# Staging the first-use weights of layer 1 in eight slots of the second residual buffer, and the flag's branch one step into the odd layer

## Chip, cores and metric

One of the eight cores of a Trainium2 chip runs the whole kernel. The metric is the device time of one execution in microseconds (us), the median of several runs. Engines are named as in the profile: PE (matrix multiplication), DVE (vector), ACT (scalar and activation), POOL (GpSimd), SP (the queue from which every DMA here is issued).

## What is computed

Two residual layers and a final norm over 2048 tokens of width 1024. Layer 0 ("even") mixes attention over the 256 keys that an index score selects with a gated convolution of 31 taps; layer 1 ("odd") is a gated convolution of 3 taps. Cut to what matters here:

```
def even_layer(h, pos, w_in, w_out, ...):
    q, k, v, qi, ki, wi, gate_a, glu_b, gate_b = _split(h @ w_in, EVEN_SPLIT)
    a = dsa_attention(rope(q), rope(k), v, rope(qi), rope(ki), wi) * silu(gate_a)
    c = silu(layer_norm(causal_depthwise_conv(g_lin * sigmoid(g_gate), cb_w))) * silu(gate_b)
    return concatenate([a, c], axis=-1) @ w_out

def odd_layer(h, w_in, conv_w, w_out):
    b_gate, c_gate, xin, gate = split(h @ w_in, 4, axis=-1)
    y = b_gate * causal_depthwise_conv(c_gate * xin, conv_w)
    return (y * silu(gate)) @ w_out

x = x + even_layer(rms_norm(x, norm_g[0]), ...)
x = x + odd_layer(rms_norm(x, norm_g[1]), ...)
return rms_norm(x, final_g)
```

## The kernel before

The tokens are worked on in four chunks of 512 (`c` = 0 to 3). A product with float32 accuracy is made of three float16 matmuls (`mm3`, lines 189 to 191): high part by high part, high by low, low by high. Each weight matrix is cut into tiles `wt` of 1024 x 256 that hold both halves; there are two `wt` buffers.

**A weight's first use.** `weight` (line 195 on) fetches a tile in four quarters of 256 KB. A quarter goes by DMA into a float32 staging tile `w_stage` (line 205, pool `stg`, two buffers), ACT scales it in place (line 210), ACT casts the high half into `wt` (line 211), and POOL subtracts to get the low half (line 212). The finished tile is also written to DRAM (line 213), and every later use is one DMA of 1 MB from there (line 199). Layer 1's input weights `wO` have 16 tiles and layer 0's output weights `woE` four; both are first used for chunk 0.

**The order of work around the change.** After layer 0's projections, gates and selection of the last chunk, the program runs for chunk 0: the last gates (`late`, lines 1122 on, in two pieces), `out_even(0)` (line 1014 on, 192 matmuls with `woE`), the norm (`norm_odd`, whose row factor `rs_d` DVE makes at line 165), and `odd(0)` (line 1050 on): 16 steps, one tile of `wO` and 48 matmuls each. `weave` runs such a main generator and, between its steps, takes so many pieces of filler generators as a rate says. Fillers are `cnv`, the 31-tap convolution of the next chunk on DVE (line 243), and `att`, the attention of the next chunk: 32 heads (4 blocks of 128 tokens, 8 heads each) and two pieces that finish the last heads, 34 pieces in all.

**One head of attention.** PE makes the scores (line 1172, `ps_q`), DVE adds the mask and takes the maximum (line 345), ACT takes the exponential (line 352) and casts (line 354), POOL subtracts (line 355, `pp`), SP issues a transposing DMA (line 357, `pt`), and PE multiplies with the values (line 378, `ps_v`). The values of a head stand two heads behind its scores.

**The branch.** All of chunk 1's attention needs the selection to be right. A flag (`fl`, `fps`, `fi`, lines 1140 to 1147) is loaded by all engines (line 1148), which branch on it (line 1149) to a slow fallback. No instruction moves across that branch. It stands after `ALONE` = 2 steps of `odd(0)`; in these steps only the convolution is woven in, and afterwards the loop at line 1186 on weaves attention at `R2` = 2.45 pieces per step into the other 14 steps.

The residual rows of a chunk, `x1` (16 KB in each partition), have two buffers in pool `l1`, used in turn; `rows` hands one out. Chunk 0 uses the first; the second stays empty until `out_even(1)`. Within what the program text allows, a scheduler orders the instructions of each engine's queue.

Of the kernel before, what the change touches and what calls it, by code (L numbers as in the profile page):

```python
# [12 lines left out]
FP32 = mybir.dt.float32  # L13
# [8 lines left out]
P = 128  # L22
S = 2048
D = 1024
KD = D // P
NB = S // P
CH = 512
# [15 lines left out]
NCAND = 16  # L43
NWT = 2
LOOK = 2
ALONE = 2
ATR = 3.5
CE, CX, CN0, CNR, R0, R1, R2 = 1.5, 3.0, 1.0, 0.85, 1.65, 1.65, 2.45
ORDER = ('ggqgqg', 'ggqgqg', 'gggg', 'qq')
EX = 1  # L50
TQ, TP = 2, 4
# [9 lines left out]
WT = 256  # L61
# [13 lines left out]
def trunk_kernel(ctx: ExitStack, tc: tile.TileContext, xT, pos, wE, woE, wO, woO, par, tab, outT):  # L75
# [40 lines left out]
    w_dr = {}  # L116
    URGENT = {(wE.tensor.name, t) for t in (T_K, T_QI, T_KI)}

    state = {"mm": None, "gate": None, "first": None, "scanned": False}

    def paced(ins):
        if state["gate"] is not None:
            tc.add_manual_dep(ins.ins, state["gate"].ins.name, mybir.DependencyInfo(mybir.DependencyClass.NoSync, mybir.DependencyReason.DATA), reason="pace")

    def drain(gen):
        for _ in gen:
            pass

    def weave(main, steps=99, *fills):
        owed = [0.0] * len(fills)  # L130
        for n, _ in enumerate(main):
            state["gate"] = state["mm"]
            for i, (gen, rate) in enumerate(fills):
                owed[i] += rate
                while owed[i] >= 1.0:
                    owed[i] -= 1.0
                    next(gen, None)
            state["gate"] = None
            if n + 1 == steps:
                break  # L140
# [13 lines left out]
    def row_rstd(pool, ps_pool, sq, inv_n, out_scale, n=TT):  # L154
        return spread(ps_pool, row_diag(pool, ps_pool, sq, inv_n, out_scale, n), n)
# [31 lines left out]
    def mm3(out, sh, sl, mh, ml):  # L187
        for k in range(KD):
            T.matmul(out=out, lhsT=sh(k), rhs=mh(k), start=k == 0, stop=False)  # L189
            T.matmul(out=out, lhsT=sh(k), rhs=ml(k), start=False, stop=False)  # L190
            state["mm"] = T.matmul(out=out, lhsT=sl(k), rhs=mh(k), start=False, stop=k == KD - 1)  # L191
        if state["first"] is None:
            state["first"] = state["mm"]

    def weight(pool, stage_pool, src, t):
        key = (src.tensor.name, t)
        wt = pool.tile([P, 2, KD, WT], F16, name="wt")
        if key in w_dr:
            SP.dma_start(out=wt, in_=w_dr[key])
            return wt  # L200
        w_dr[key] = dram.tile([P, 2, KD, WT], F16, name=f"w_{key[0]}_{t}")
        for q in range(4):
            ks = slice(2 * q, 2 * q + 2)
            st = stage_pool.tile([P, 2, WT], FP32, name="w_stage")
            SP.dma_start(out=st, in_=src[t, :, ks, :])
            if key in URGENT:
                A.activation(out=wt[:, 0, ks, :], in_=st, func=AF.Copy, scale=SW)
                paced(V.scalar_tensor_tensor(out=wt[:, 1, ks, :], in0=st, scalar=SW, in1=wt[:, 0, ks, :], op0=ALU.mult, op1=ALU.subtract))
            else:
                A.activation(out=st, in_=st, func=AF.Copy, scale=SW)  # L210
                A.copy(out=wt[:, 0, ks, :], in_=st)  # L211
                G.tensor_tensor(out=wt[:, 1, ks, :], in0=st, in1=wt[:, 0, ks, :], op=ALU.subtract)  # L212
        SP.dma_start(out=w_dr[key], in_=wt)
        return wt
# [212 lines left out]
    with ExitStack() as es:  # L427
# [482 lines left out]
        def score_slot(i, n):  # L910
            return scp.tile([P, n, CH], FP32, name=f"sc{i}", padded_shape=[P, n, -(-(NB - TT + i + 1) * P // n)])
# [34 lines left out]
        a, b, d = score_slot(3, 4), score_slot(0, 3), score_slot(1, 3)  # L946
# [6 lines left out]
        x1 = first_normalize(1, acc, held)  # L953
# [31 lines left out]
    l1 = ctx.enter_context(tc.tile_pool(name="l1", bufs=2, reuse_waits="tile"))  # L985
# [52 lines left out]
    def halves():  # L1038
        return xp.tile([P, KD, CH], F16, name="xh"), xp.tile([P, KD, CH], F16, name="xl")
# [42 lines left out]
    def out_odd(c, x1, yh, yl, parts=1):  # L1082
        acc = l1.tile([P, CH], FP32, name="ssum", bufs=1)
        w = CH // parts
        for n in range(parts):
            tok = slice(n * w, (n + 1) * w)
            for t in range(NTW):
                wt = weight(wp, stg, woO, t if n % 2 == 0 else NTW - 1 - t)
                for z in range(2):
                    jt = 2 * (t if n % 2 == 0 else NTW - 1 - t) + z  # L1090
                    zs = slice(z * P, (z + 1) * P)
                    ps = ps_w.tile([P, CH], FP32, name="ps_w")[:, 0:w]
                    mm3(ps, lambda k: wt[:, 0, k, zs], lambda k: wt[:, 1, k, zs], lambda k: yh[:, k, tok], lambda k: yl[:, k, tok])
                    x = x1[:, jt, tok]
                    V.scalar_tensor_tensor(out=x, in0=ps, scalar=1.0 / (SY * SW), in1=x, op0=ALU.mult, op1=ALU.add)
                    square_into(l1, acc[:, tok], x, t + z == 0, V)
                yield
            rb = row_rstd(l1, ps_n, acc[:, tok], 1.0 / D, 1.0, w // P)
            for k in range(0, KD, parts):
                o = l1.tile([P, CH], FP32, name="y" if parts > 1 and k // parts % 2 else "xi").rearrange("p (z t) -> p z t", z=parts)  # L1100
                for z in range(parts):
                    V.scalar_tensor_tensor(out=o[:, z, :], in0=x1[:, k + z, tok], scalar=gf[:, k + z:k + z + 1], in1=rb[:, 0:w], op0=ALU.mult, op1=ALU.mult)  # L1102
                rows = outT[k * P:(k + parts) * P, c * CH + n * w:c * CH + (n + 1) * w]
                SP.dma_start(out=rows.rearrange("(z p) t -> p z t", z=parts), in_=o)

    m = {}

    def rows():
        return l1.tile([P, KD, CH], FP32, name="x1"), l1.tile([P, CH], FP32, name="ssum", bufs=1)

    def last_gates():
        xh, xl = held_last
# [8 lines left out]

    late = last_gates()
    x1, acc = rows()
    weave(late, LG)
    for z in range(2):
        SP.dma_start(out=mix(0)[z][:, 4:8, :], in_=mc_dr[:, z])
# [6 lines left out]
    n = norm_odd(x1, acc, late)  # L1133
    drain(late)
    yh, yl = halves()
    main = odd(*n, yh, yl)
    weave(main, ALONE, (cnv, CN0))

# [54 lines left out]
    for c in range(NCH):  # L1193
        att = attend(c + 1) if c + 1 < NCH else iter(())
        if c > 0:
            cnv = conv(c + 1) if c + 1 < NCH else iter(())
            x1, acc = rows()
            weave(out_even(c, *m[c], x1, acc), 99, (cnv, CNR), (att, R0))
            n = norm_odd(x1, acc, late, (cnv, CNR), (att, R1))
            weave(late, 99, (cnv, CNR), (att, R1))  # L1200
            yh, yl = halves()
            main = odd(*n, yh, yl)
        weave(main, 99, (cnv, CNR if c else CN0), (att, R1 if c else R2))
        late = out_odd(c, x1, yh, yl, 2 if c + 1 == NCH else 1)
        drain(att)
        drain(cnv)
# [71 lines left out]
```

## Time and profile before

| | |
|---|---|
| runs | 2228.39, 2229.94, 2234.19 us; median 2229.94 |
| profiled execution | 2226.34 us, of which the profile spans 2224.6 |
| PE | 1988.8 us busy (89%), mean granted clock 0.97 |
| DVE, ACT, POOL | 1659.4 (75%), 1177.1 (53%), 803.5 us (36%) |
| `w_stage<-in_wo_dram` | 64 DMAs of 256 KB, median 3.3 us from issue to landing |
| `pt<-pp` | 320 transposing DMAs, median 3.3 us |

PE is busy for nine tenths of the span, but in the page's row of 40 slices its share falls to 7 and 8 tenths in slices 18 to 21 (about 1000 to 1220 us), which are `odd(0)` and what follows on it. A busy share is a mean over stages with different limits, so this stretch is to be read by itself: which engine waits, for what, and what lies ahead of it in the queues.

### The profile page before, as it was taken

How to read it: one execution, taken by the hardware profiler on the slowest of the kernel's cores; microseconds unless marked ns; L12 is line 12 of the kernel's file. 1: busy time of each engine (PE TensorE's matmuls, PEld its weight loads, DVE VectorE, ACT ScalarE, POOL GpSimd, SP SyncE). 2: the span in 40 equal slices, each digit the busy share in tenths (PEclk: the TensorE clock that was granted, in tenths of full speed). 3: DMA queues.
4: the chain of work that ended last, by engine and by line, in shares of the span. 5: the costliest groups of instructions: out<-in, count | busy, mean ns of one | idle time of the engine just before them, and what ended most of it. 6: DMA issues, size and time to landing. Idle time of an engine off the chain costs nothing. (4 is left out here: it accounts for less than half of the span.)

```text
span 2224.6 us, 34871 instructions
## 1 busy us (share of the span) xinstructions
PE 1988.8 (89%) x12252; PEld 1071.2 (48%) x12252; DVE 1659.4 (75%) x3485; ACT 1177.1 (53%) x2407; POOL 803.5 (36%) x761
## 2 busy tenths in 40 slices
PE   5778888888999998897877999999999999999997
PEld 4644464555464543343433444554444555444446
DVE  7999969998988867887662887875788887343224
ACT  5666666566567855465673564554455567121111
POOL 4765343534142503244643442442343455000000
PEclk9889999999999999898988999999999999999999
DMA  6445447334645475566776677785678888433234
GB/s 230 170 160 207 170 172 234 105 104 164 190 121 165 126 254 198 175 196 177 189 196 178 175 207 192 169 199 155 164 174 193 196 177 180 140 112 139 95 102 164
DMA packets 405475, 378.79 MB, mean 170 GB/s; under 512 B 313392, under 2 KB 333616, under 8 KB 384560
## 3 DMA queue, kind: packets, MB, share of 16 engines
q1 hardware_dynamic: 405296, 376.54, 59.0%
q8 instruction: 96, 1.57, 0.3%
q14 instruction: 83, 0.68, 0.1%
HBM read 214.35 MB, written 88.70 MB: 136 GB/s over the span
## 5 line engine op out<-in xcount | busy, mean ns | idle before, releaser
L355 POOL TENSOR_TENSOR pp<-lg,pp 128x512 f16<-128x512 f32 (+3 forms) x320 | 339.7, 1084 | 617.6 <-ACT pp L354 531.4
L189 PE MATMUL ps_w<-xh,wt 128*128 128x512 f16 (+1 forms) x1376 | 514.3, 375 | 26.3 <-ACT wt L211 18.8
L190 PE MATMUL ps_w<-xl,wt 128*128 128x512 f16 (+1 forms) x1376 | 514.6, 374 | 0.2 <-DVE xl L185 0.2
L191 PE MATMUL ps_w<-xh,wt 128*128 128x512 f16 (+1 forms) x1376 | 508.9, 374 | 4.6 <-POOL wt L212 4.6
L189 PEld LDWEIGHTS <-wt 128*128 128x128 f16 x2112 | 209.5, 99 | 257.0 <-ACT wt L211 25.5
L190 PEld LDWEIGHTS <-wt 128*128 128x128 f16 x2112 | 209.1, 99 | 246.0 <-issue 34.1
L191 PEld LDWEIGHTS <-wt 128*128 128x128 f16 x2112 | 208.9, 99 | 246.2 <-POOL wt L212 18.6
L243 DVE SCALAR_TENSOR_TENSOR ps_c<-cin,cwt,ps_c 128x512 f32<-128x512 f32 x348 | 261.2, 751 | 23.9 <-ACT ps_c L241 19.4
L352 ACT ACTIVATE lg<-lg,m 128x512 f32<-128x512 f32 (+3 forms) x320 | 207.0, 648 | 135.0 <-DVE m L345 134.6
L212 POOL TENSOR_TENSOR wt<-w_stage,wt 128x512 f16<-128x512 f32 x136 | 166.4, 1229 | 261.3 <-ACT wt L211 233.8
L189 PE MATMUL ps_p<-xh,wt 128*128 128x512 f16 x480 | 185.0, 386 | 13.9 <-ACT th L224 7.2
L191 PE MATMUL ps_p<-xh,wt 128*128 128x512 f16 x480 | 183.7, 384 | 1.4 <-POOL wt L212 1.4
L190 PE MATMUL ps_p<-xl,wt 128*128 128x512 f16 x480 | 184.3, 384 | 0.0
L741 DVE SCALAR_TENSOR_TENSOR sc<-relu,wi,sc 128x1024 f32<-128x1024 f32 (+7 forms) x140 | 164.5, 1175 | 14.2 <-ACT relu L739 14.1
L737 PE MATMUL ps_i<-ki,qst 128*128 128x512 f16 (+3 forms) x608 | 146.6, 358 | 31.9 <-ACT relu L739 30.3
L739 ACT ACTIVATE relu<-ps_i 128x1024 f32<-128x1024 f32 (+7 forms) x176 | 142.1, 809 | 61.8 <-DVE sc L741 48.1
L354 ACT CAST pp<-lg 128x512 f16<-128x512 f32 (+3 forms) x320 | 163.9, 547 | 18.4 <-DMA pt<-pp 16.4
L189 PE MATMUL ps_p<-wt,xh 128*128 128x256 f16 (+1 forms) x608 | 164.3, 270 | 5.2 <-ACT u L596 2.3
L190 PE MATMUL ps_p<-wt,xh 128*128 128x256 f16 (+1 forms) x608 | 164.3, 270 | 0.0
L191 PE MATMUL ps_p<-wt,xl 128*128 128x256 f16 (+1 forms) x608 | 163.4, 270 | 0.5 <-DVE xl L491 0.3
L378 PE MATMUL ps_v<-vv,pt 128*128 128x64 f16 (+1 forms) x2016 | 116.9, 209 | 37.2 <-DMA pt<-pp 37.0
L792 ACT ACTIVATE junk<-sc,t_x 128x640 bf16<-128x640 f32 (+5 forms) x84 | 118.7, 1413 | 59.4 <-DVE t_x L807 45.8
(285 smaller groups left out, 3497.1 us busy)
## 6 DMA issues: line engine op xcount, KB each, us to landing
wt<-w_in_wo_dram SPq DMA_DIRECT2D x48, 1024.0 KB, 5.0
wt<-w_in_we_dram SPq DMA_DIRECT2D x39, 1024.0 KB, 5.4
w_stage<-in_wo_dram SPq DMA_DIRECT2D x64, 256.0 KB, 3.3
w_in_wo_dram<-wt SPq DMA_DIRECT2D x16, 1024.0 KB, 5.1
wt<-w_in_woo_dram SPq DMA_DIRECT2D x16, 1024.0 KB, 4.8
w_in_we_dram<-wt SPq DMA_DIRECT2D x13, 1024.0 KB, 5.2
w_stage<-in_we_dram SPq DMA_DIRECT2D x48, 256.0 KB, 3.1
wt<-w_in_woe_dram SPq DMA_DIRECT2D x12, 1024.0 KB, 4.9
```

The lines of the kernel that those rows point to most:

```text
L189: T.matmul(out=out, lhsT=sh(k), rhs=mh(k), start=k == 0, stop=False)
L190: T.matmul(out=out, lhsT=sh(k), rhs=ml(k), start=False, stop=False)
L191: state["mm"] = T.matmul(out=out, lhsT=sl(k), rhs=mh(k), start=False, stop=k == KD - 1)
L212: G.tensor_tensor(out=wt[:, 1, ks, :], in0=st, in1=wt[:, 0, ks, :], op=ALU.subtract)
L243: ins = V.scalar_tensor_tensor(out=out if t == CK - 1 else acc, in0=ci[:, t:t + CH], scalar=cwt[:, j, t:t + 1], in1=acc, op0=ALU.mult, op1 ...
L352: A.activation(out=e, in_=e, func=AF.Exp, bias=last, scale=-1.0, accum_out=blk["ss"][:, h, si:si + 1])
L354: A.copy(out=pp[:, 0:w], in_=e)
L355: eng.tensor_tensor(out=pp[:, w:2 * w], in0=e, in1=pp[:, 0:w], op=ALU.subtract)
L737: T.matmul(out=ps[:, r0:r0 + r], lhsT=qst[:, h, i * P:(i + 1) * P], rhs=ki[:, a, s0 + r0:s0 + r0 + r], start=a == 0, stop=a == 1)
L739: A.activation(out=rl[:, 0:w], in_=ps[:, 0:w], func=AF.Relu)
L741: V.scalar_tensor_tensor(out=sc[:, s0:s0 + w], in0=rl[:, 0:w], scalar=wi[:, b, h:h + 1], in1=tiny[:, s0:s0 + w] if h == 0 else sc[:, s0:s0 ...
L792: A.activation(out=junk[:, 0:W], in_=sc, func=AF.Sign, bias=x[:, n:n + 1], scale=-1.0, accum_out=cn[:, n:n + 1])
```

## The change

It does four things. `spare` takes the second `x1` buffer out of the pool at the start of layer 1, and `rows` hands that same tile to chunk 1 later. Until `odd(0)` is done, `weight` stages in that tile instead of in `w_stage`: `stage_in` cuts it into eight slots of the size of a staging tile, used in turn. `ALONE` falls from 2 to 1, so that the flag and the branch stand one step earlier. `R2` falls from 2.45 to 2.3, over 15 steps instead of 14 (34.5 pieces instead of 34.3).

```
-ALONE = 2
+ALONE = 1
-CE, CX, CN0, CNR, R0, R1, R2 = 1.5, 3.0, 1.0, 0.85, 1.65, 1.65, 2.45
+CE, CX, CN0, CNR, R0, R1, R2 = 1.5, 3.0, 1.0, 0.85, 1.65, 1.65, 2.3
...
-            st = stage_pool.tile([P, 2, WT], FP32, name="w_stage")
+            st = state["stage"]() if state["stage"] else stage_pool.tile([P, 2, WT], FP32, name="w_stage")
...
+    spare = []
+
     def rows():
-        return l1.tile([P, KD, CH], FP32, name="x1"), l1.tile([P, CH], FP32, name="ssum", bufs=1)
+        x1 = spare.pop() if spare else l1.tile([P, KD, CH], FP32, name="x1")
+        return x1, l1.tile([P, CH], FP32, name="ssum", bufs=1)
+
+    def stage_in(x):
+        slots = x.rearrange("p (n a) t -> p n (a t)", n=KD)
+        turn = [0]
+
+        def slot():
+            turn[0] += 1
+            return slots[:, turn[0] % KD, :].rearrange("p (k w) -> p k w", k=2)
+
+        return slot
...
     x1, acc = rows()
+    spare.append(l1.tile([P, KD, CH], FP32, name="x1"))
+    state["stage"] = stage_in(spare[0])
     weave(late, LG)
...
         weave(main, 99, (cnv, CNR if c else CN0), (att, R1 if c else R2))
+        state["stage"] = None
         late = out_odd(c, x1, yh, yl, 2 if c + 1 == NCH else 1)
```

The queues of all engines are the same as before up to the last gates, and again from chunk 1's `out_even` on. Between them they are ordered anew. Three places follow; `x_9788` in them is the spare `x1` tile.

POOL in the middle of `odd(0)`, before:

```order
L212 TENSOR_TENSOR wt<-w_stage,wt 128x512
L355 TENSOR_TENSOR pp<-lg,pp 128x512
L355 TENSOR_TENSOR pp<-lg,pp 128x256
L355 TENSOR_TENSOR pp<-lg,pp 128x512
L212 TENSOR_TENSOR wt<-w_stage,wt 128x512
L355 TENSOR_TENSOR pp<-lg,pp 128x256
```

and with the change:

```order
L251 TENSOR_TENSOR cn_s<-cn_s,cv 128x512
L212 TENSOR_TENSOR wt<-x_9788,wt 128x512 x4
L355 TENSOR_TENSOR pp<-lg,pp 128x512
L355 TENSOR_TENSOR pp<-lg,pp 128x256
```

The subtractions of a tile's four quarters, which stood singly between those of attention, now stand four in a row, and so do ACT's casts of line 211.

ACT at the end of `odd(0)` (line 1076 is its last activation, lines 352 and 354 are attention's), before:

```order
L1076 ACTIVATE th_14290<-ps_w 128x512
L352 ACTIVATE lg,ss_a<-lg,m_14296 128x512 x2
L184 CAST xh<-y 128x512
L210 ACTIVATE w_stage<-w_stage 128x512
L354 CAST pp<-lg 128x512 x2
L385 COPY a_nat<-ps_v 128x256
```

and with the change:

```order
L352 ACTIVATE lg,ss_a<-lg,m_14141 128x512 x2
L354 CAST pp<-lg 128x512 x2
L1076 ACTIVATE th_14250<-ps_w 128x512
L385 COPY a_nat<-ps_v 128x256
L184 CAST xh<-y 128x512
```

The last head's exponentials now stand ahead of the last step's activation. On PE, 29 matmuls of the odd layer and 32 small ones of attention (line 378) follow behind the last scores; before, the last scores came behind the last matmul of the odd layer.

ACT at the end of the selection (line 792 is the selection's count), where `woE`'s first tile is converted, before:

```order
L211 CAST wt<-w_stage 128x512 x2
L792 ACTIVATE junk,t_cn<-sc_7336,t_x 128x1920
L1063 COPY cx<-halo 128x2
L792 ACTIVATE junk,t_cn<-sc_7466,t_x 128x2048
L210 ACTIVATE w_stage<-w_stage 128x512
L224 ACTIVATE th_9815<-ps_w 128x512
L210 ACTIVATE w_stage<-w_stage 128x512
L211 CAST wt<-w_stage 128x512 x2
L792 ACTIVATE junk,t_cn<-sc_7336,t_x 128x1920
L792 ACTIVATE junk,t_cn<-sc_7466,t_x 128x2048
```

and with the change:

```order
L792 ACTIVATE junk,t_cn<-sc_7466,t_x 128x2048
L210 ACTIVATE x_9788<-x_9788 128x512 x3
L224 ACTIVATE th_9816<-ps_w 128x512
L210 ACTIVATE x_9788<-x_9788 128x512
L211 CAST wt<-x_9788 128x512 x3
L792 ACTIVATE junk,t_cn<-sc_7336,t_x 128x1920
L211 CAST wt<-x_9788 128x512
L210 ACTIVATE x_9788<-x_9788 128x512 x3
L224 ACTIVATE th_9847<-ps_w 128x512
L210 ACTIVATE x_9788<-x_9788 128x512
L792 ACTIVATE junk,t_cn<-sc_7466,t_x 128x2048
```

Between the two last pairs of counts there were five instructions; now fourteen stand ahead of the last count.

## Rows read from the trace of the kernel before

**Rows 1.** Stretches: length, busy us of PE, PEld, DVE, ACT, POOL; clock, DMA share, GB/s.

```profile
921.00:945.80 24.80, 24.30 (x103) 10.54 (x103) 22.18 (x32) 12.30 (x23) 5.17 (x5) 0.90 0.44 154
945.80:1198.00 252.20, 205.98 (x1221) 98.04 (x1218) 171.91 (x325) 160.69 (x368) 130.29 (x120) 0.94 0.73 197
1198.00:1209.30 11.30, 2.83 (x21) 2.14 (x22) 1.97 (x5) 1.89 (x4) 2.26 (x2) 0.54 0.45 129
1310.00:1560.00 250.00, 243.35 (x1559) 124.79 (x1558) 186.50 (x371) 125.18 (x298) 86.75 (x79) 0.99 0.72 179
1810.00:1860.00 50.00, 50.00 (x362) 27.00 (x361) 39.69 (x84) 32.12 (x75) 29.81 (x25) 1.00 0.96 190
```

**Rows 2.** Who waited for whom, PE, 921 to 1209.3 us.

```profile
PE ps_v L378 <- DMA pt<-pp: 21.3, 10, 8.1
PE ps_w L189 <- ACT wt L211: 18.8, 10, 4.9
PE ps_w L191 <- POOL wt L212: 4.6, 9, 1.1
```

**Rows 3.** Instructions on w_stage, 945.8 to 1209.3 us; ns min/median/max.

```profile
L210 ACT ACTIVATE w_stage<-w_stage x53: 612/629/634, 948.4 to 1197.2; 128x512 f32<-128x512 f32 x53
L211 ACT CAST wt<-w_stage x52: 600/613/619, 945.3 to 1188.9; 128x512 f16<-128x512 f32 x52
L212 POOL TENSOR_TENSOR wt<-w_stage,wt x52: 1143/1157/1681, 947.6 to 1189.6; 128x512 f16<-128x512 f32 x52
...
DMA to landing us min/median/max: 2.4/3.5/7.2
```

**Rows 4.** Who waited for whom, ACT, 945.8 to 1209.3 us.

```profile
ACT w_stage L210 <- DMA w_stage<-in_wo_dram: 37.7, 21, 5.3
```

**Rows 5.** PE in order of time; columns: start, us, engine, line, operation, [idle before <-releaser].

```profile
1009.88 0.61 PE L189 MATMUL ps_w<-xh,wt 128*128 128x512 f16 x1 [3.91 <-ACT wt L211]
...
1048.29 0.61 PE L189 MATMUL ps_w<-xh,wt 128*128 128x512 f16 x1 [3.36 <-ACT wt L211]
...
1128.49 0.61 PE L189 MATMUL ps_w<-xh,wt 128*128 128x512 f16 x1 [4.85 <-ACT wt L211]
...
1133.59 0.59 PE L190 MATMUL ps_w<-xl,wt 128*128 128x512 f16 x1
...
1134.01 0.38 PE L191 MATMUL ps_w<-xh,wt 128*128 128x512 f16 x1
```

**Rows 6.** All engines in order of time, end of the stretch.

```profile
1192.54 1.03 PE L1172 MATMUL ps_q<-kk,qs_a 128*128 128x512 f16 x4
...
1203.01 0.82 PE L378 MATMUL ps_v<-vv,pt 128*128 128x128 f16 x8 [8.09 <-DMA pt<-pp]
...
1209.23 1.01 PE L189 MATMUL ps_w<-mh,wt 128*128 128x512 f16 x2 [1.43 <-ACT mh L184]
```

**Rows 7.** ACT in order of time, end of the selection.

```profile
848.77 1.12 ACT L211 CAST wt<-w_stage 128x512 f16<-128x512 f32 x2
849.79 1.90 ACT L792 ACTIVATE junk<-sc,t_x 128x1920 bf16<-128x1920 f32 x1
```

**Rows 8.** DVE in order of time, same place.

```profile
853.94 0.16 DVE L797 SCALAR_TENSOR_TENSOR t_d<-t_cn,t_wc 128x2 f32<-128x2 f32 x1 [4.63 <-ACT junk L792]
```

**Rows 9.** Who waited for whom, 842 to 921 us.

```profile
PE ps_m L171 <- DVE rs_d L165: 5.5, 1, 5.5
...
DVE ssum L181 <- ACT sq L180: 1.7, 2, 1.0
```

**Rows 10.** DVE in order of time, at the branch.

```profile
945.57 0.15 DVE L1147 TENSOR_SCALAR fi<-ps_m 128x1 int32<-128x1 f32 x1
...
950.47 0.69 DVE L1077 SCALAR_TENSOR_TENSOR th<-th,ps_w 128x512 f32<-128x512 f32 x1 [4.03 <-DVEq L1149]
```

**Rows 11.** Instructions on pt, 945.8 to 1209.3 us.

```profile
DMA to landing us min/median/max: 2.3/3.3/7.5
```

**Rows 12.** Instructions on pt, 1810 to 1860 us.

```profile
DMA to landing us min/median/max: 2.9/3.6/7.2
```

More of the change, by code (lines that the diff above doesn't have):

```diff
@@ L117, in trunk_kernel @@
     URGENT = {(wE.tensor.name, t) for t in (T_K, T_QI, T_KI)}
-    state = {"mm": None, "gate": None, "first": None, "scanned": False}
+    state = {"mm": None, "gate": None, "first": None, "stage": None, "scanned": False}
     def paced(ins):
```

## Prediction

> **What bounds the kernel now.** I read the page's row of slices first, to find where PE is not full: about 1000 to 1220 us. Then the table by stretch. From 945.8 us (the branch) to 1198 PE is busy 206 of 252 us at a clock of 0.94, and in the 11.3 us after that 2.8 us at 0.54; the same layer for chunk 1, 1310 to 1560, has PE busy 243 of 250 us at 0.99 [rows 1]. The difference between the two is where the weights come from: chunk 0 converts them, chunk 1 reads them back finished. DVE is busy 172 of the 252 us, ACT 161, POOL 130 and the DMA engines 0.73 of the time, so none of them is full; the stretch is bound by waits.
>
> Which waits, the view of waits says. From 921 us, where the odd layer begins, to 1209.3, where chunk 1's `out_even` begins, PE waits 18.8 us in ten places for ACT's casts of a weight, 4.6 us in nine for POOL's subtractions, and 21.3 us in ten for `pt`, attention's transposed probabilities [rows 2]. Why the weights are late is seen on ACT: 37.7 us in 21 waits of line 210 for the DMA of a quarter [rows 4]. A quarter takes 3.5 us to land, then 0.63, 0.61 and 1.16 us on ACT, ACT and POOL [rows 3], 5.9 in all; with two staging tiles that is at best 2.95 us a quarter or 11.8 us a tile, before any of the queues is late. And since ACT works in order, its 37.7 us also hold up attention's exponentials.
>
> What a stall costs beyond itself is in the timeline: after the wait of 4.85 us the matmuls stand 0.425 us apart (12 spacings from 1128.49 to 1133.59 us), with durations of 0.59 to 0.63 us, and at 1134.01 they are back at 0.38 [rows 5]. These are the two levels of PE's clock, 1.2 and 2.4 GHz; at the full one I take half the spacing, 0.21 us, so 48 matmuls of a step are 10.2 us.
>
> **The change, part by part.**
>
> *Eight slots.* The same 64 quarters of `wO` and 16 of `woE` are loaded, scaled, cast and subtracted, at the same durations, so no engine gets work or loses it; what changes is when the loads may start. Loads and scaling for two tiles can run ahead. What must still wait for a free `wt` buffer is four casts and four subtractions: 0.61 + 4 x 1.16 = 5.3 us, while PE has 10.2 us of the other tile to do. That fits by 5 us a step even where ACT or POOL is a little late. Of 18.8 + 4.6 = 23.4 us of waits [rows 2] I leave 2: **-21.4 us**; the bounds are 0 and -23.4. The quarters of `out_even(0)` come earlier as well, but I cost that at nothing: DVE is what ends that stretch (below).
>
> *The clock behind these stalls.* The three longest, 3.91, 3.36 and 4.85 us [rows 5], are each followed by matmuls at the lower level. Behind the last, 12 spacings cost 12 x 0.21 = 2.5 us more than at full speed; in proportion to the stalls the other two cost 2.0 and 1.7. Together **-6.2 us**, bounds 0 and -6.2.
>
> *The end of the odd layer.* Before, the last head's scores stand behind PE's last matmul of the layer (1192.54 us), and PE then waits 8.09 us for `pt`, with nothing left to cover it; `out_even(1)` starts at 1209.23 at the lower level [rows 6]. In the new order 29 matmuls of the layer (6.2 us) stand behind the last scores, and the exponentials no longer stand behind line 1076. I take **-6 us**, bounds -2 and -8.1. The way from the last values to `out_even(1)` (a transpose, two passes of DVE, a cast) stays.
>
> *The end of the selection.* Here the change costs. ACT's last count of the selection now has nine more conversions ahead of it, at a spacing of 0.51 us (848.77 to 849.79 for two [rows 7]): 4.6 us. DVE waits for that count already, 4.63 us [rows 8], and from there to `rs_d` it is busy almost without a break, while PE waits 5.5 us for `rs_d`. So the delay goes through to the norm, less what DVE can make up: the 1.7 us that it waited for ACT's squares [rows 9] in between. I take **+3 us**, bounds 0 and +4.6. It also says why a faster `out_even(0)` gains nothing.
>
> *The branch.* Its stop on DVE, from 945.57 to 950.47 with 4.03 us idle [rows 10], is paid as before, at a place one step earlier. PE has matmuls queued across it in both. The step that it passes keeps its 48 matmuls and its convolution; attention starts that much sooner and is spread over 15 steps, 2.3 pieces instead of 2.45 in each. No term: 0, within -4 and +4.
>
> *Attention's waits inside the layer.* 21.3 - 8.1 = 13.2 us. Two things pull on them. ACT is rid of its DMA waits, so the exponentials come sooner. But a step of PE gets shorter, so the two heads between scores and values cover less, and POOL's four subtractions in a row put 4 x 1.16 = 4.6 us ahead of a `pp` that comes at the wrong moment. I leave 13.2 as it is, **0**; all of it gone is -13, one more such 4.6 us in every third step +23.
>
> Here a rule of the skill is to be weighed. Every transfer of this stretch is in SP's queue, weights and transposes alike, and the four loads of a tile are now issued close together. The transposes do not seem to mind a full queue: the median from issue to landing is 3.3 us in this stretch [rows 11], and 3.6 us from 1810 to 1860 [rows 12], where the DMA share is 0.96 and PE is busy for all 50 us [rows 1]; so I add nothing. The Trainium skill ("DMA: Bandwidth & Descriptors", section Queues, rings and completion order) states that each DMA engine consumes the descriptors of a queue in ring order, so by that rule a transpose stands behind every load issued before it. By the rows the sum has no term for it; by the rule it would have the one of the third rival.
>
> **Sum.** -21.4 - 6.2 - 6 + 3 = -30.6, say -31 us against the profiled execution's 2226.34: 2195. The median of the runs is 3.6 us above that execution (2229.94), and I carry the same distance over: **2199 us**. Everything behind 1209 us has the same queues as before, so the gain is neither given back nor added to there.
>
> **Rivals.**
>
> 1. *Waits for `pt` take the place of those for weights.* The step gets shorter, the chain of attention does not. For it: `pt` is already PE's longest wait [rows 2], and the fours on POOL. Against: ACT's 37.7 us of blocked queue go. If each of 15 steps waits 1.6 us more, 24 of the 31 us are gone: gain 7, 2223 us.
> 2. *The stretch becomes like chunk 1's.* If attention profits from ACT's free queue, PE could reach the 243/250 = 0.973 of 1310 to 1560. PE's busy time from 921 on is 24.3 + 206.0 + 2.8 = 233.1 us [rows 1], which at 0.973 is 240 instead of 288: -48 + 3 = -45, 2185 us. Against: chunk 0 still converts weights on ACT and POOL.
> 3. *Slower: transposes queue behind the bursts of loads.* Three quarters are 0.79 MB, at this stretch's 197 GB/s [rows 1] 4.0 us. If a transpose that PE is about to need stands behind such a burst in each of 15 steps, that is +60 - 31 = +29: 2259 us. It decides from 31 / 15 = 2.1 us a step. Against it: rows 11 and 12 as above, and the number of bytes is the same. The rule named above is this case's.
> 4. *The slots do nothing*, since the two `wt` buffers were the limit all along. Then only the end and the selection count, -6 + 3: 2227 us. Against it: ACT's waits of line 210 name the DMA of a quarter, and not PE [rows 4].
>
> **How the numbers follow.** Chances: the forecast 0.69, rival 1 0.10, rival 2 0.12, rival 3 0.05, rival 4 0.04. The forecast's own range, with the waits of attention 10 us either way and the other bounds, is 2188 to 2213. The range that I give reaches on the low side past rival 2, to 2181, and on the high side to 2218, short of rivals 1, 3 and 4, which hold 0.19. About 0.3%, or 6.7 us, is what a measurement of this kernel can tell from no change. Rival 1 lies just on that bound, so half of it counts as the same, with rival 4: same 0.09, slower 0.05, faster 0.86.
>
> **What would show it.** Right: hardly any wait of PE for casts or subtractions of weights between the branch and chunk 1's `out_even`, no wait of line 210 for DMAs to speak of, a stretch of some 255 to 260 us instead of 288 from the first odd matmul to `out_even(1)`, its clock at 0.96 or more, a last wait for `pt` of about 2 us, and `rs_d` some 3 us later than 915. Rival 1 shows as waits for `pt` of 35 us and more, rival 3 as a median landing time of `pt` well above 3.6 us. The forecast is wrong if waits of casts remain (then for PE's release of `wt`, rival 4), or if DVE's first part moves by much more than 5 us.

## The result and the profile after

The change takes 2196.35 us (median of 4 runs, 2191.58 to 2199.44) against 2229.16 us before (4 runs): a ratio of 0.9847, with an interval of 0.9823 to 0.9872. The forecast was 2199.0 us within 2181 to 2218. The time is right to 2.7 us, but the odd layer gained 10 us more than forecast, the way to it lost 7 us more, and what follows on it took 7 us more: that the total is so close is in part luck.

| | before | after |
|---|---|---|
| profiled execution, span | 2226.34, 2224.6 us | 2196.97, 2195.2 us |
| PE busy | 1988.8 us (89%) | 1990.9 us (91%) |
| fifth count of the selection to `rs_d` | 839.62 to 914.76: 75.1 us | 838.58 to 924.07: 85.5 us |
| first matmul of the odd layer to `out_even(1)` | 920.92 to 1209.23: 288.3 us | 928.44 to 1173.24: 244.8 us |
| from there to the end of the span | 1015.4 us | 1022.0 us |

The odd layer is 43.5 us shorter, the way to it 10 us longer, and what follows 6.6 us longer. First the odd layer, in the table by stretch of the kernel before (length, busy us of PE, PEld, DVE, ACT, POOL; clock, DMA share, GB/s; the same columns as [rows 1]):

```profile
921.00:1209.20 288.20, 233.03 (x1342) 110.65 (x1342) 195.97 (x359) 174.88 (x393) 137.72 (x127) 0.92 0.69 191
```

and of the change:

```profile
942.20:1162.00 219.80, 202.35 (x1229) 100.97 (x1228) 177.06 (x332) 159.24 (x370) 140.38 (x124) 0.98 0.86 219
1162.00:1173.20 11.20, 7.14 (x65) 4.17 (x64) 4.18 (x9) 3.04 (x6) 2.27 (x2) 1.00 0.96 231
928.40:1173.20 244.80, 223.11 (x1342) 110.88 (x1342) 193.75 (x359) 167.38 (x383) 142.65 (x126) 0.97 0.82 210
```

PE does the same 1342 matmuls in 223.11 us instead of 233.03, because its clock is granted at 0.97 instead of 0.92 of full speed; the rest of the gain is idle time, 21.7 us instead of 55.2. Who waited for whom on PE in the same stretch of the change:

```profile
PE ps_v L378 <- DMA pt<-pp: 10.5, 10, 3.3
PE ps_m L402 <- DVE a_nat L398: 5.2, 2, 3.5
PE ps_q L1187 <- DVE m L345: 3.5, 4, 1.1
PE ps_w L189 <- ACT xh L184: 1.5, 1, 1.5
```

Against [rows 2], all waits for casts (18.8 us) and for subtractions of weights (4.6 us) are gone, and those for `pt` are halved. At the end of the layer, PE in order of time (start, us, idle before), against [rows 6]:

```profile
1168.98 0.51 PE L378 MATMUL ps_v<-vv,pt 128*128 128x64 f16 x8 [0.52 <-DMA pt<-pp]
1171.15 0.66 PE L402 MATMUL ps_m<-id,a_nat 128*128 128x128 f32 x4 [1.65 <-DVE a_nat L398]
1173.24 1.01 PE L189 MATMUL ps_w<-mh,wt 128*128 128x512 f16 x2 [1.43 <-ACT mh L184]
```

The wait of 8.09 us for the last `pt` is 0.52 us. ACT still waits for quarters (against [rows 4]):

```profile
ACT x L210 <- DMA x<-in_wo_dram: 24.6, 19, 2.7
```

That is 24.6 us of 37.7; but with the lead over PE that eight slots give, no matmul waits for a weight. Landing times of `pt` in this stretch (against [rows 11]):

```profile
DMA to landing us min/median/max: 2.3/3.7/8.3
```

DVE's stop at the branch is 2.34 us instead of the 4.03 of [rows 10].

Now the way to the odd layer. DVE of the change in order of time, at the selection's last step (before, the wait was 4.63 us, [rows 8]):

```profile
846.33 0.16 DVE L796 TENSOR_TENSOR t_dx<-t_x 128x2 f32<-128x2 f32 x1
858.08 0.69 DVE L1023 SCALAR_TENSOR_TENSOR x<-ps_w,xi 128x512 f32<-128x512 f32 x1 [11.60 <-PE ps_w L191]
858.69 0.88 DVE L797 SCALAR_TENSOR_TENSOR t_d<-t_cn,t_wc 128x2 f32<-128x2 f32 x1
859.60 1.08 DVE L798 TENSOR_TENSOR t<-t_d 128x2 f32<-128x2 f32 x1
860.72 1.08 DVE L799 SCALAR_TENSOR_TENSOR t_d<-t,t_d 128x2 f32<-128x2 f32 x1
861.84 1.08 DVE L802 SCALAR_TENSOR_TENSOR t_g<-t_d 128x2 f32<-128x2 f32 x1
862.95 0.17 DVE L803 RECIPROCAL t_g<-t_g 128x2 f32<-128x2 f32 x1
```

The residual add of `out_even(0)` (line 1023) stands ahead of the last step, and it waits 11.60 us for PE's first 24 matmuls with `woE`. PE itself waited for the first cast, and then ran at the lower clock:

```profile
849.35 0.61 PE L189 MATMUL ps_w<-mh,wt 128*128 128x512 f16 x1 [2.78 <-ACT wt L211]
...
855.68 0.42 PE L191 MATMUL ps_w<-mh,wt 128*128 128x512 f16 x1
855.94 0.38 PE L189 MATMUL ps_w<-mh,wt 128*128 128x512 f16 x1
```

Between the first two of these rows there are 13 matmuls, some 0.42 us apart; from the third on they stand 0.21 to 0.22 apart.

And then four operations on 128 x 2 numbers took 0.88 to 1.08 us each; one step earlier they took 0.16. POOL, in the same time:

```profile
858.39 4.51 POOL L212 TENSOR_TENSOR wt<-x,wt 128x512 f16<-128x512 f32 x4 [4.43 <-ACT wt L211]
```

The last step needs ACT's last count as well. ACT's read of that count, before:

```profile
853.72 0.19 ACT L792 ACTIVATION_READ_ACCUMULATOR junk<-sc,t_x 128x1 f32 x1
```

and with the change, behind a wait for a quarter of `woE` that stands in ACT's queue ahead of it:

```profile
847.16 0.63 ACT L210 ACTIVATE x<-x 128x512 f32<-128x512 f32 x1 [1.46 <-DMA x<-in_woe_dram]
...
857.10 0.19 ACT L792 ACTIVATION_READ_ACCUMULATOR junk<-sc,t_x 128x1 f32 x1
```

Before, DVE's last step began as soon as this read was done, at 853.94. With the change the read was done at 857.29, and the step began at 858.69. So of DVE's 11.60 us of waiting, all but 0.8 would have been waited for ACT alone; the residual add put 1.4 us on top (that 0.8 and its own 0.6). These 1.4 us matter twice: begun at 857.29, the four operations would have been over, at 0.2 us each, before POOL's row began at 858.39.

### The profile page after: what moved, and what is told of

Its sections match the earlier page's. It is cut to its first block, busy times and chain, and to the rows that moved or that the text cites. A ratio compares the mean times of both kernels' runs of the same rounds, so it can differ in the third digit from the quotient of the medians.

```text
span 2195.2 us, 34791 instructions
## 1 busy us (share of the span) xinstructions
PE 1990.9 (91%) x12252; PEld 1076.5 (49%) x12252; DVE 1663.6 (76%) x3485; ACT 1174.1 (53%) x2407; POOL 806.0 (37%) x761
## 5 line engine op out<-in xcount | busy, mean ns | idle before, releaser
L190 PEld LDWEIGHTS <-wt 128*128 128x128 f16 x2112 | 209.2, 99 | 247.4 <-issue 33.8
L189 PE MATMUL ps_p<-wt,xh 128*128 128x256 f16 (+1 forms) x608 | 167.2, 275 | 4.6 <-ACT u L596 2.5
L190 PE MATMUL ps_p<-wt,xh 128*128 128x256 f16 (+1 forms) x608 | 167.2, 275 | 0.0
L212 POOL TENSOR_TENSOR wt<-x,wt 128x512 f16<-128x512 f32 x80 | 98.6, 1264 | 149.2 <-ACT wt L211 124.8
L1187 PE MATMUL ps_q<-kk,qs_a 128*128 128x512 f16 (+3 forms) x576 | 140.1, 353 | 9.4 <-DVE m L345 9.4
```

Of the source, the lines that this page charges most:

```text
L1187: ins = T.matmul(out=ps[:, 0:w], lhsT=qs[:, h, :], rhs=kk[:, a, s0:s0 + w], start=a == 0, stop=a == 1)
```

## Experiments

The table sums up the readings; the sections after it tell of each kernel. Each stretch is from that kernel's profile: the selection's fifth count on DVE to `rs_d`, the odd layer from its first matmul to `out_even(1)`, and the rest of the span. The ratios are to runs of the kernel before on the same chip, whose medians were 2228.7 to 2231.6 us; a difference between medians from two chips can be off by as much (3 us).

| kernel | count to `rs_d` | odd layer | rest | median, us | ratio to before (interval) |
|---|---|---|---|---|---|
| before | 75.1 | 288.3 | 1015.4 | 2229.16 | 1 |
| branch_only | 75.5 | 272.8 | 1018.0 | 2214.24 | 0.9932 (0.9908 to 0.9956) |
| slots2 | 76.8 | 270.9 | 1018.9 | 2214.72 | 0.9935 (0.9912 to 0.9958) |
| slots_only | 83.3 | 251.0 | 1019.6 | 2200.34 | 0.9873 (0.9846 to 0.9899) |
| late_265 | 85.4 | 247.4 | 1015.1 | 2194.61 | 0.9858 (0.9829 to 0.9888) |
| early_245 | 86.9 | 245.7 | 1018.1 | 2194.89 | 0.9840 (0.9808 to 0.9872) |
| the change | 85.5 | 244.8 | 1022.0 | 2196.35 | 0.9847 (0.9823 to 0.9872) |
| same_after | 86.5 | 245.9 | 1020.0 | 2199.70 (one run) | |
| odd_slots | 79.9 | 243.7 | 1017.6 | 2188.67 | 0.9820 (0.9794 to 0.9845) |
| slots4 | 79.1 | 239.4 | 1017.7 | 2183.17 | 0.9799 (0.9772 to 0.9827) |
| odd_psum | 76.6 | 240.7 | 1014.6 | 2180.28 | 0.9784 (0.9759 to 0.9809) |
| slots4_psum | 78.1 | 236.7 | 1013.8 | 2177.85 | 0.9764 (0.9744 to 0.9783) |
| odd4_psum | 75.9 | 242.7 | 1013.8 | 2177.80 | 0.9755 (0.9736 to 0.9775) |
| before_psum | 74.6 | 287.4 | 1011.2 | 2225.49 | 0.9974 (0.9960 to 0.9988) |

### Which edit carries the gain: slots_only and branch_only

slots_only is the change with two lines put back, branch_only the kernel before with the same two lines changed:

```
slots_only:   ALONE = 2 ... R2 = 2.45   (in the change)
branch_only:  ALONE = 1 ... R2 = 2.3    (in the kernel before)
```

> The eight slots as in the change, but flag and branch after two steps as before (ALONE 2, R2 2.45). Theory: the slots carry the whole gain, the branch is worth nothing: 2196 us within 5, no waits of PE for casts or subtractions of weights in the odd layer of chunk 0, and the norm's row factor rs_d as late as in the change, at about 924 us. Rival: the branch's earlier place carries part of the gain, then 2203 us or more.

> The kernel before with ALONE 1 and R2 2.3 alone, weights staged in the two tiles of before. Theory: no gain without slots, 2229 us within 5, with waits of 15 to 25 us for casts. Rival: attention that starts a step sooner shortens the end of the layer by itself, 2221 us or less, and the last wait for pt falls from 8 us to under 4.

slots_only took 2200.34 us. It has no waits for casts in the odd layer, and `rs_d` comes at 922.9 us: this part is as the theory said, and the total lies in its range. But branch_only took 2214.24, 14.5 us less than the kernel before on its chip (2228.69), where the theory wanted none: its rival was right. So two edits that gain 14.5 us (branch_only) and 28 us (slots_only) alone gain 33 us together: the gains don't add up. The last values of the odd layer, in slots_only

```profile
1171.97 0.82 PE L378 MATMUL ps_v<-vv,pt 128*128 128x128 f16 x8 [7.49 <-DMA pt<-pp]
```

and in branch_only

```profile
1187.85 0.51 PE L378 MATMUL ps_v<-vv,pt 128*128 128x64 f16 x8 [0.55 <-DMA pt<-pp]
```

show what the branch's move and the new rate bring. With the slots alone, the last scores still stand behind PE's last matmul of the layer, and PE waits 7.49 us for the last `pt`, nearly the 8.09 of before. With the move alone, matmuls of the layer lie between, and the wait is 0.55 us. branch_only's waits in the odd layer are these:

```profile
PE ps_w L189 <- ACT wt L211: 11.5, 10, 3.0
PE ps_v L378 <- DMA pt<-pp: 10.9, 10, 1.8
PE ps_w L191 <- POOL wt L212: 6.8, 11, 1.4
```

So of 15.5 us, 10.4 are waits for `pt`, 5.1 are waits for weights (23.4 became 18.3), and 3.4 are PE's busy time, less some new waits. Beside the slots the move is worth 6.2 us of the odd layer (251.0 to 244.8).

### Position of the branch or rate of the weaving: late_265 and early_245

```
late_265:   ALONE = 2 ... R2 = 2.65   (in the change)
early_245:  ALONE = 1 ... R2 = 2.45   (in the change)
```

> The eight slots with flag and branch after two steps as before, but attention woven at 2.65 pieces per step instead of 2.45: the last head's scores now stand ahead of the layer's last matmuls, as in the change. Theory: what the branch's move gave beside the slots is only that the last heads are finished inside the layer; so the rate does it alone: the last wait for pt falls from 7.5 us to under 2 and the total to 2190 to 2198 us. Rival: the earlier branch matters by its longer stretch for attention; then denser attention costs as much as the end gains, 2199 us or more.

> As the change (eight slots, branch after one step), with attention at 2.45 pieces per step instead of 2.3: the last values stand ahead of the layer's last three matmuls. Theory: the end gains 2 to 3 us more (its wait for the last pt and the a_nat behind it lie beside matmuls), 2191 to 2196 us. Rival: the denser weaving brings waits for pt and for DVE's maxima inside the layer, 2197 us or more.

late_265 took 2194.61 us, inside the theory's range, and no `pt` is waited for at the end; the first wait of PE's there is

```profile
1173.23 0.66 PE L402 MATMUL ps_m<-id,a_nat 128*128 128x128 f32 x4 [1.00 <-DVE a_nat L398]
```

So the rate does it, with the branch where it was: what counts is that the last head's scores come early enough to have matmuls behind them. The rates agree with this: the pieces of attention that are due before the last step are 13 x 2.45 = 31.85 in the kernel before, one short of the 32 heads, but 14 x 2.3 = 32.2 in the change and 13 x 2.65 = 34.5 in late_265. early_245 took 2194.89 us, inside the theory's numbers, but its odd layer (245.7 us) is no shorter than the change's; the 1.5 us between the medians lie within the spread of the runs. In its profile both sides show: PE waits 1.0 us for `a_nat` instead of 5.2, as the theory wanted, and 14.2 us for `pt` instead of 10.5, as the rival did.

### How many slots: slots2 and slots4

```
-            return slots[:, turn[0] % KD, :]...
+            return slots[:, turn[0] % 4, :]...    (slots4; % 2 in slots2)
```

> As the change, but the slots of the second residual buffer are used two in turn, as many as before. Theory: it is the number that counts, not the place: as with the branch's move alone, 2214 us within 6, with 10 us or more of waits for casts in the odd layer. Rival: the new place or the orders that come with it give the gain, 2200 us or less.

> As the change, but the slots are used four in turn, not eight: one weight tile ahead instead of two. DVE's residual add stands behind the selection's last step here too. Theory: one tile ahead nearly does, since four casts and four subtractions need 5.3 us of a step's 10.2; PE waits under 6 us for casts in the odd layer, rs_d at 916 to 919 us, total 2188 to 2198 us. Rival: the lead over two tiles is what hides the loads, then 10 us or more of waits for casts and 2200 us or more.

slots2 took 2214.72 us, the same as branch_only, with 14.2 us of waits for casts and 5.5 for subtractions: the place of the slots is worth nothing, their number is. slots4 took 2183.17 us, 5 us less than the lowest that the theory allowed, and 13 us less than the change (11 by the ratios). PE does not wait for one weight there, so four slots give all the lead that is needed. Its way to `rs_d` is 6.4 us shorter than the change's: ACT's last count is done 17.1 us after the fifth instead of 18.7, and DVE's residual add stands behind the selection's last step (1.4 us), which so is over when POOL's row begins at 859.39 (3.5 us). The step waits for ACT alone:

```profile
857.28 0.16 DVE L797 SCALAR_TENSOR_TENSOR t_d<-t_cn,t_wc 128x2 f32<-128x2 f32 x1 [9.20 <-ACT junk L792]
```

9.20 against the 4.63 of [rows 8]: this is the cost of ACT's queue by itself, 4.6 us. At `rs_d` 3.9 us are seen (79.1 against 75.1), but not because DVE makes up for a part. The kernel before lost 1.8 us one step earlier, in two small operations beside two subtractions of POOL (840.66 to 842.93), which take 0.16 us in slots4 and in the change:

```profile
840.80 1.03 DVE L805 TENSOR_TENSOR t_g<-t_g,t_gmin 128x2 f32<-128x2 f32 x1
841.86 1.08 DVE L806 TENSOR_TENSOR t_g<-t_d,t_g 128x2 f32<-128x2 f32 x1
```

And behind the last step slots4 needs 60.2 us to `rs_d`, the kernel before 59.1: 4.6 - 1.8 + 1.1 = 3.9.

### Putting the selection right: odd_slots

```
-            st = state["stage"]() if state["stage"] else stage_pool.tile(...)
+            st = state["stage"]() if state["stage"] and src is wO else stage_pool.tile(...)
```

> As the change, but woE's quarters stay in the two w_stage tiles; only wO is staged in the eight slots. In the change DVE's first residual add stands ahead of the selection's last step and waits 11.6 us; here the order of before is back. Theory: rs_d comes back from 924 to about 915 us, the odd layer stays at 245 us (245 to 250), so some 9 us less than the change: 2187 us (2183 to 2192). Rival: what is won at the selection is lost by a later start of the odd layer's first weights, 2194 to 2199 us, with rs_d at 915 but casts waited for.

The slots of the change take the four tiles of `woE` too, which are weights of layer 0; here they don't. It took 2188.67 us, 7.7 less than the change, as the theory said in total (6 by the ratios, whose intervals overlap). But `rs_d` came at 921.3, not at 915 (79.9 us after the fifth count, not 75.1). DVE had lost its time at another place, in the reciprocal root of the norm:

```profile
916.48 0.16 DVE L149 TENSOR_TENSOR rs_t<-rs_r 128x4 f32<-128x4 f32 x1
916.67 1.02 DVE L150 SCALAR_TENSOR_TENSOR rs_t<-rs_t,rs_a 128x4 f32<-128x4 f32 x1
917.73 1.08 DVE L151 SCALAR_TENSOR_TENSOR rs_r<-rs_t,rs_r 128x4 f32<-128x4 f32 x1
918.84 1.07 DVE L149 TENSOR_TENSOR rs_t<-rs_r 128x4 f32<-128x4 f32 x1
919.95 1.08 DVE L150 SCALAR_TENSOR_TENSOR rs_t<-rs_t,rs_a 128x4 f32<-128x4 f32 x1
921.06 0.16 DVE L151 SCALAR_TENSOR_TENSOR rs_r<-rs_t,rs_r 128x4 f32<-128x4 f32 x1
921.26 0.69 DVE L165 SCALAR_TENSOR_TENSOR rs_d<-id,rs_r 128x512 f32<-128x512 f32 x1
```

beside four subtractions of POOL, now those of `wO`'s first tiles:

```profile
916.52 4.49 POOL L212 TENSOR_TENSOR wt<-x,wt 128x512 f16<-128x512 f32 x4 [6.95 <-ACT wt L211]
```

### What slows DVE's small operations: odd_psum and before_psum

The root is rewritten so that its running value `at` lies in PSUM (unused columns of `ps_m`); each operation then reads one operand from there and one from SBUF.

```
+            V.tensor_copy(out=at, in_=r)
             for _ in range(steps):
-                V.tensor_tensor(out=t, in0=r, in1=r, op=ALU.mult)
-                V.scalar_tensor_tensor(out=t, in0=t, scalar=-0.5, in1=a, ...)
-                V.scalar_tensor_tensor(out=r, in0=t, scalar=1.5, in1=r, ...)
+                V.tensor_tensor(out=t, in0=at, in1=a, op=ALU.mult)
+                V.scalar_tensor_tensor(out=t, in0=t, scalar=-0.5, in1=at, ...)
+                V.scalar_tensor_tensor(out=at, in0=t, scalar=1.5, in1=at, ...)
```

> As odd_slots (woE in w_stage, wO in eight slots), with the reciprocal root of the norms written so that each small operation of DVE reads one operand from PSUM and one from SBUF instead of two from SBUF. In odd_slots four of these operations took 1.02 to 1.08 us instead of 0.16, beside four subtractions of POOL in a row (4.49 us), and rs_d was made 5.97 us after rs_a. Theory: DVE operations with two SBUF operands wait for POOL's; with one they don't: all of them take 0.15 to 0.25 us, rs_d comes 2.2 to 2.8 us after rs_a, the odd layer starts some 3.5 us sooner, total 2183 to 2187 us. Rival: the operations are slow for another reason (their queue, their data), then they take over 0.8 us here too and the total is 2187 to 2191 us.

> The kernel before with the norms' reciprocal root reading one operand from PSUM, and nothing else. In the kernel before the small operations of these roots sum to 52.4 us (153 of them, up to 1.24 us each), against 25 at 0.16 us. Theory: part of the 27 us lies on the path (the norms in which PE waits for rs_d), 3 to 10 us less: 2219 to 2226 us. Rival: with POOL's subtractions single, as in the kernel before, the wait for POOL is beside other work, 2226 to 2230 us.

In odd_psum the same stretch of DVE reads

```profile
916.03 0.16 DVE L152 SCALAR_TENSOR_TENSOR rs_t<-rs_t,ps_m 128x4 f32<-128x4 f32 x1
916.22 0.17 DVE L153 SCALAR_TENSOR_TENSOR ps_m<-rs_t,ps_m 128x4 f32<-128x4 f32 x1
916.42 0.16 DVE L151 TENSOR_TENSOR rs_t<-ps_m,rs_a 128x4 f32<-128x4 f32 x1
...
917.60 0.69 DVE L172 SCALAR_TENSOR_TENSOR rs_d<-id,ps_m 128x512 f32<-128x512 f32 x1
```

with POOL just as busy beside it:

```profile
915.72 4.49 POOL L219 TENSOR_TENSOR wt<-x,wt 128x512 f16<-128x512 f32 x4 [7.07 <-ACT wt L218]
```

No operation takes over 0.17 us. Over the whole span of odd_slots, by the view of one tile (ns min/median/max), the old root's second operation reads

```profile
L150 DVE SCALAR_TENSOR_TENSOR rs_t<-rs_t,rs_a x51: 151/161/1239, 17.7 to 2178.1; 128x4 f32<-128x4 f32 x45, 128x2 f32<-128x2 f32 x6
```

and in odd_psum its counterpart

```profile
L152 DVE SCALAR_TENSOR_TENSOR rs_t<-rs_t,ps_m x51: 143/157/159, 17.5 to 2169.6; 128x4 f32<-128x4 f32 x45, 128x2 f32<-128x2 f32 x6
```

The theory holds for these operations: what slowed them was a second operand from SBUF while POOL worked on SBUF. The total, 2180.28 us, lies under the theory's range. It is 8.4 us under odd_slots, more than the 3.6 us of this one chain; the odd layer starts only 2.5 us sooner. The other norms gain too, as the rest of the span shows: 1011.2 to 1014.6 us in the four kernels with the new root, 1015.1 to 1022.0 in the ten profiles with the old one. In the kernel before, grouped by line over the whole span (columns: count, then busy us and mean ns), these operations stand as

```profile
L150 DVE SCALAR_TENSOR_TENSOR rs_t<-rs_t,rs_a 128x4 f32<-128x4 f32 (+1 forms) x51 | 19.4, 381 | 1.4
...
L149 DVE TENSOR_TENSOR rs_t<-rs_r 128x4 f32<-128x4 f32 (+1 forms) x51 | 18.2, 358 | 1.2
...
L151 DVE SCALAR_TENSOR_TENSOR rs_r<-rs_t,rs_r 128x4 f32<-128x4 f32 (+1 forms) x51 | 14.8, 291 | 1.2
```

and with the new root, in before_psum, as

```profile
L153 DVE SCALAR_TENSOR_TENSOR ps_m<-rs_t,ps_m 128x4 f32<-128x4 f32 (+1 forms) x51 | 8.4, 164 | 1.4
...
L151 DVE TENSOR_TENSOR rs_t<-ps_m,rs_a 128x4 f32<-128x4 f32 (+1 forms) x51 | 8.1, 159 | 1.4
...
L152 DVE SCALAR_TENSOR_TENSOR rs_t<-rs_t,ps_m 128x4 f32<-128x4 f32 (+1 forms) x51 | 7.9, 155 | 1.4
```

52.4 us became 24.4, and the 17 copies that the new root adds are 2.9 (0.17 each). before_psum took 2225.49 us against 2231.63 for the kernel before on that chip, 6 us less; the interval (0.12 to 0.40% faster) leaves out no change.

The Trainium skill ("SBUF — State Buffer", section Who interferes with whom) states that a DVE instruction with two SBUF inputs contends with a GpSimd instruction that reads SBUF, and that the one that comes second is blocked until the first is done. The trace agrees: the slowed operations stand 1.11 us apart, one for each of POOL's subtractions (4.49 us for four), and with one of their two inputs in PSUM they are not slowed.

One SBUF input alone is not enough for every operation. The root begins with two operations of another kind (TENSOR_SCALAR, lines 146 and 147), which read one operand from SBUF and write there; they were left as they are. In odd_psum one of them reads

```profile
1100.52 1.08 DVE L147 TENSOR_SCALAR rs_r<-rs_r 128x4 int32<-128x4 int32 x1
```

beside the last of three subtractions:

```profile
1097.73 3.85 POOL L219 TENSOR_TENSOR wt<-x,wt 128x512 f16<-128x512 f32 x3
```

Its median over the span is 0.17 us.

### The parts that did best together: slots4_psum and odd4_psum

```
slots4_psum:  slots4 with the root of odd_psum
odd4_psum:    odd_psum with turn[0] % 4
```

> Four slots in turn for woE and wO (as slots4, 2183 us) with the norms' reciprocal root reading one operand from PSUM (as odd_psum). In slots4 the small operations before rs_d already take 0.15 to 0.16 us, so the stretch from the selection to the odd layer has nothing to gain; elsewhere in the kernel the three forms of these operations sum to 50.1 us, and would to some 25. Theory: only the other norms gain, 1 to 6 us: 2177 to 2182 us. Rival: the gain of odd_psum was that one chain of 3.7 us alone, then 2182 to 2185 us.

> woE in w_stage, wO in four slots in turn, the root reading PSUM: the parts that did best put together. Theory: the selection's last step is as early as in odd_slots (855 us against 857 in slots4) and the odd layer as short as with four slots (239 against 244 us), so 2 to 4 us less than odd_psum: 2176 to 2179 us. Rival: four and eight slots do the same in the odd layer once woE is out of them (their difference of 4 us is the kernel's own spread), 2179 to 2183 us.

Both took 2177.8 us, 18.5 us less than the change: they are the fastest of this study, and cannot be told apart. Both totals lie in the theory's ranges. In slots4_psum the reason holds for the most part: against slots4 the rest of the span is 3.9 us shorter, but the odd layer is 2.7 us shorter as well. In odd4_psum it does not: the odd layer is 242.7 us, no shorter than with eight slots (240.7), so once `woE` is out of the slots, four and eight do the same there. Among the kernels in which PE waits for no weight, the odd layer takes 236.7 to 251.0 us. slots_only's 251.0 has the wait at its end in it; what makes the difference between 237 and 247 among the others was not settled. (Of the 10.7 us between slots4_psum and late_265, 6.5 are PE's busy time, 219.9 against 226.4 us, at a granted clock of 0.98 against 0.93.)

### Whether the gain is given back behind chunk 1: same_after

The change unaltered, once more.

> The change again, for a second profile: what lies behind chunk 1's out_even took 1022.0 us in the first profile, against 1015.4 before, though the queues are the same. Theory: spread between executions, some 1015 to 1020 us here. Rival: the change makes that part slower, 1021 us or more again.

The rest of the span took 1020.0 us. PE's order there is the same in all ten profiles of kernels with the old root, and they spread from 1015.1 to 1022.0, with the kernel before near the low end and the change at the high one. So most of the 6.6 us is spread between executions. The two profiles of the change (1022.0, 1020.0) are the two highest, so a loss of some 2 us there can't be excluded.

## Why the prediction was right, and where it was not

| step of the sum | forecast | measured |
|---|---|---|
| waits for weights | -21.4 | -23.4: none left |
| clock | -6.2 | -9.9: PE's busy time, 233.03 to 223.11 |
| end of the odd layer | -6 | -7.6: last wait 8.09 to 0.52 |
| waits of attention inside | 0 | +3: `pt` -3.2, `a_nat` +3.6, DVE's maxima +2.6 |
| other waits in the odd layer | not in the sum | -7.8: `rs_d` -3.8, `xh` -1.8, `th` and `y` -1.8, `cn_q` -0.4 |
| end of the selection | +3 | +10.3 |
| way from `rs_d` to the first matmul | not in the sum | -1.8 |
| behind `out_even(1)` | 0 | +6.6, mostly spread |

The first five terms, those of the odd layer, add up to -45.7, and the layer is 43.5 us shorter; the 2.2 us are the views' own difference, for the waits on PE's list sum to 58.4 and 22.7 us where its busy time leaves 55.2 and 21.7 idle. With the other three (+10.3, -1.8, +6.6), and 1.0 us by which this profile was ahead at the selection's fifth count, -43.5 makes -29.4 us: the difference of the spans.

**Waits for weights.** Right, and the slots are what does it: with two slots in the same place 19.7 us remain, with four or eight none. The working was right too: two tiles' loads ahead of PE leave only casts and subtractions to be done in a step. That four slots do as well was not seen. The telltale "no wait of line 210 to speak of" was wrong: 24.6 us of them are left, and PE waits for no weight, because the lead covers them. (Whether they delay attention's exponentials, which are in ACT's queue too, was not tried.)

**Clock.** Right in kind, under-sized. I priced only the matmuls behind the three longest stalls; over the layer as a whole the granted clock rose from 0.92 to 0.97.

**End of the layer and branch.** The end's -6 was right (-7.6), but I put it to "the new order" and costed the branch at nothing. slots_only, branch_only and late_265 show that the slots have no part in it: what brings it is the rate at which attention is woven, by which the last scores stand ahead of the last matmuls. By itself that edit gains 14.5 us, where my term for it said 0 within 4. The sum came out right because the gain was priced once, under another name.

**End of the selection.** This step failed. It said that ACT's last count has nine conversions more ahead of it (eight, and an activation of line 224), 4.6 us, of which 3 go through to the norm, and its upper bound was 4.6; 10.3 were measured. The prediction's own sign of being wrong, DVE's first part moving by much more than 5 us, came true here. The price of the nine holds, but four things were left out. One of them waits 1.5 us for a load of `woE`, in ACT's queue ahead of the count: the count comes 6.2 us later behind the step before it, not 4.6. DVE's own queue moved as well, and I looked at ACT's only: the residual add stands ahead of the last step, +1.4. By that the step ran into POOL's row of subtractions, and four small operations lost 3.5 us (0.88 + 3 x 1.08 less 4 x 0.16). And DVE made up for nothing: from the last step's end to `rs_d` it took 1.1 us more, though its wait for ACT's squares went from 1.7 us to none. Less the 1.8 us that only the kernel before lost one step earlier, 6.2 + 1.4 + 3.5 + 1.1 - 1.8 = 10.4, against 10.3 measured.

**The rivals.** Rival 1 (waits for `pt` take the place) did not come: they were halved. Rival 2 was nearer in the odd layer's time, 244.8 us where it said 240 and the forecast 255 to 260, but not by its mechanism: PE is busy 0.91 of the layer, not 0.973, and 9.9 us came from the clock. The selection's extra loss and the spread behind hid that in the total, which is where luck had a part. Rival 3 (transposes behind bursts of loads) did not come: at a DMA share of 0.86 instead of 0.73 the median landing time of `pt` rose from 3.3 to 3.7 us, not by 4.0, and PE's longest wait for one inside the layer is 3.3 us. Whether the rule of the Trainium skill weighed there ("DMA: Bandwidth & Descriptors", section Queues, rings and completion order) holds here, no run shows. Rival 4 (the `wt` buffers are the limit) is excluded by the waits for weights, which went to nothing with two `wt` buffers.

## What to carry to other kernels

When a change lets one engine run ahead, read the new order of every engine whose queue is shared with the critical chain before pricing the delay: here ACT's row of instructions told 4.6 us of 10.3, and the rest came from a load that ACT waited for, from DVE's own order and from a row of POOL's beside it. Buffer as far ahead as the longest wait needs and no further: two slots left 19.7 us of waits for weights, four left none, and eight only let a scheduler put more early work in front of what was urgent. The 13 us between four and eight are not all explained by that. By the two profiles 6.4 us lie at the selection; 5.4 in the odd layer were not settled, 4.3 behind it are within the spread, and with `woE` out of the slots four and eight differ by 2.5 us. And put an edit's gain to that edit: "the branch" and "the slots" were one term each, and only kernels with one of them showed whose the gain was.

## What was not expected of the hardware

A DVE operation on 128 x 4 or 128 x 2 numbers that reads two operands from SBUF took 0.88 to 1.08 us instead of 0.16 in the rows above, beside POOL's subtractions of 1.16 us, and at most 1.24 us, beside a POOL operation of 1.87 us (line 181, at 67 us); with one of the operands in PSUM, none of 153 took over 0.17 us. (POOL's longest subtraction of weights in the change took 2.07 us where the median is 1.16; whether DVE held it up was not tried.) So subtractions that a scheduler puts in a row on POOL cost a chain of small DVE operations one subtraction per operation: 3.5 us in the change, 3.6 in odd_slots.
